# Splitting the first load of a streaming kernel between two issuing engines

## The chip, the cores and the metric

The kernel runs on one core of a Trainium2 chip. The time is the device time of one execution in microseconds, the median of three runs. The profile is one further execution, recorded by the hardware profiler; its span is a little shorter than the device time (167.1 us against 168.98 us for the same execution).

The engines are named as the profile names them: PE is TensorE, with PEld its weight loads, DVE is VectorE, ACT is ScalarE, POOL is GpSimd, and SP is SyncE, which issues the loads. A "q" after an engine's name means its instruction queue.

## The reference

For an input of 32 x 512 rows of 1024 positive numbers, the result is the sum of the reciprocals of each row:

```python
def setup_inputs():
    batch, seq, dim = 32, 512, 1024
    return {"x": np.abs(np.random.randn(batch, seq, dim)).astype(np.float32) + 1e-6}

def reference(x):
    return np.sum(1.0 / x, axis=-1).astype(np.float32)
```

The input is 67.1 MB, the output 64 KB.

## The kernel before

The 16384 rows are spread over 128 partitions, 128 rows each. A row is halved, and two numbers share one reciprocal: 1/a + 1/b = (a + b) x 1/(ab). GpSimd (or VectorE) makes the products, ScalarE makes the reciprocal as exp(-ln), TensorE or the reducing instruction makes the sums, and VectorE multiplies and reduces. A ring of 40 rows per partition holds the input; a hand-made list, PLAN, sets the order of everything. `D4` in it is a load of the next four rows, `D8` of the next eight, and so on.

```python
P = 128; D = 1024; H = D // 2; F = 128; R = 40
PLAN = """
    D4 D8 D15 D13 P0+2 C3@3 S2@0 V3 P2 L0@0 L1@1 C11@3 S3@1 E0@6 E1@7 P4+2 V11 L2@3 L3@2
    R0 S6@2 E2 E3 R1 P6+2 ...                          # cut
""".split()

x_v = x.flatten_outer_dims().rearrange("(p f) d -> p f d", p=P)

act_sets = list(get_activation_tables(nc.m.arch).keys())
nc.scalar.add_instruction(mybir.InstLoadActFuncSet(...))   # cut: ln and exp in one table
...
ring = pool.tile([P, R, D], f32)
...
with tc.manual_schedule():
    for op, r, n, b in ops:
        if op == "D":
            n, r = r, loaded
            while n:
                q, at, w = place(r)
                a = q % R
                m = min(n, R - a, LAST - r) if r < LAST else 1
                inst = nc.sync.dma_start(
                    out=ring[:, a : a + m, at : at + 2 * w],
                    in_=x_v[:, q : q + m, at : at + 2 * w],
                )
                note("SP", inst, writes=rows(r, m))
                r, n = r + m, n - m
            loaded = r
        elif op == "P":      # products on GpSimd, reads the ring
        elif op == "C":      # TensorE copies half a row to PSUM
        elif op in "WV":     # products on VectorE
        elif op == "S":      # TensorE adds the two halves of a row into PSUM
        elif op == "L":      # ScalarE: ln
        elif op == "E":      # ScalarE: exp
        elif op == "R":      # VectorE: multiply and reduce; frees the row of the ring
        # cut
    nc.sync.dma_start(out=out_v, in_=sums)
```

`note` records what an instruction reads and writes, and leaves out a wait that other waits already imply:

```python
def note(engine, inst, reads=(), writes=()):
    ...                                               # cut: finds earlier users of the same rows
    for other in needed:
        o_inst, o_engine, o_tick, _, _, o_known = other
        if o_engine == engine:
            continue
        if o_tick <= known.get(o_engine, 0):
            tc.declare_no_dep(inst, o_inst, reason="implied by other waits")
            continue
        for e, t in o_known.items():
            known[e] = max(known.get(e, 0), t)
        known[o_engine] = max(known.get(o_engine, 0), o_tick)
```

In the built program the loads use eight completion semaphores in turn, so a load also waits until the earlier load with the same semaphore has landed.

Of the kernel before, what the change touches and what calls it, by code (L numbers as in the profile page):

```python
# [11 lines left out]
def kernel(  # L12
# [5 lines left out]
    nc = tc.nc  # L18
    f32 = mybir.dt.float32
    P = 128  # L20
# [58 lines left out]
    x_v = x.flatten_outer_dims().rearrange("(p f) d -> p f d", p=P)  # L79
    out_v = out.flatten().rearrange("(p f) -> p f", p=P)  # L80

    act_sets = list(get_activation_tables(nc.m.arch).keys())
    nc.scalar.add_instruction(  # L83
        mybir.InstLoadActFuncSet(
            name=nc.get_next_instruction_name(),
            act_func_set_id=act_sets.index("natural_log_exp_and_others"),
            ins=[],
            outs=[],
        )
    )  # L90

    pool = ctx.enter_context(tc.tile_pool(name="pool", bufs=1))
    pspool = ctx.enter_context(
        tc.tile_pool(name="pspool", bufs=1, space=bass.MemoryType.PSUM)
# [1 line left out]
    ring = pool.tile([P, R, D], f32)  # L96
# [15 lines left out]
    def place(r):  # L112
        if r < LAST:
            return r, 0, H
        part, q = divmod(r - LAST, F - LAST)
        return LAST + q, part * H, H // 2

    def xs(r, h):
        q, at, w = place(r)
        return ring[:, q % R, at + h * w : at + (h + 1) * w]  # L120

    loaded = 0
# [10 lines left out]
    def note(engine, inst, reads=(), writes=()):  # L133
        inst = inst.ins
        known = dict(begun.get(engine, {}))
        before = {}
        for spaces, writing in ((reads, False), (writes, True)):
            for space in spaces:
                for other in history.get(space, ()):
                    if writing or other[3]:  # L140
                        before[other[0].name] = other
        needed = sorted(before.values(), key=lambda o: -o[4])
# [4 lines that stand above are left out]
            if o_tick <= known.get(o_engine, 0):  # L147
                tc.declare_no_dep(inst, o_inst, reason="implied by other waits")
                continue
            for e, t in o_known.items():  # L150
                known[e] = max(known.get(e, 0), t)
            known[o_engine] = max(known.get(o_engine, 0), o_tick)
        count[engine] = count.get(engine, 0) + 1
        begun[engine] = known
        entry = (engine, count[engine])
        if engine == "SP":
            entry = (f"load {count[engine]}", 1)
        for spaces, writing in ((reads, False), (writes, True)):
            for space in spaces:
                history.setdefault(space, []).append(  # L160
                    (inst, *entry, writing, sum(count.values()), known)
                )

    def rows(r, n, h=None):
        spaces = []
        for q, at, w in (place(i) for i in range(r, r + n)):
            end = at + 2 * w
            if h is not None:
                at, end = at + h * w, at + (h + 1) * w
            spaces += [("row", q % R, i) for i in range(at, end, H // 2)]  # L170
        return spaces

    def slots(r, n):
        return [("slot", pslot[q]) for q in range(r, r + n)]

    with tc.manual_schedule():
        for op, r, n, b in ops:
            p = pslot.get(r)
# [3 lines that stand above are left out]
                    q, at, w = place(r)  # L182
                    a = q % R
                    m = min(n, R - a, LAST - r) if r < LAST else 1
                    inst = nc.sync.dma_start(  # L185
                        out=ring[:, a : a + m, at : at + 2 * w],
                        in_=x_v[:, q : q + m, at : at + 2 * w],
                    )
                    note("SP", inst, writes=rows(r, m))
                    r, n = r + m, n - m  # L190
                loaded = r
            elif op == "P":
                while n:
                    q, at, w = place(r)
                    a, p = q % R, pslot[r]
                    m = min(n, R - a)
                    inst = nc.gpsimd.tensor_tensor(  # L197
                        out=prod[:, p : p + m, :w],
                        in0=ring[:, a : a + m, at : at + w],
                        in1=ring[:, a : a + m, at + w : at + 2 * w],  # L200
                        op=mult,
                    )
                    note("POOL", inst, rows(r, m), slots(r, m))
                    r, n = r + m, n - m
            elif op == "C":
                copied[r] = b
                inst = nc.tensor.matmul(  # L207
                    ps[:, b, : place(r)[2]],
                    lhsT=ident,
                    rhs=xs(r, 1),  # L210
                    start=True,
                    stop=True,
                )
                note("PE", inst, rows(r, 1, 1), [("bank", b)])
            elif op in "WV":
                w = place(r)[2]
                in1 = xs(r, 1) if op == "W" else ps[:, copied[r], :w]
                inst = nc.vector.tensor_tensor(  # L218
                    out=prod[:, p, :w], in0=xs(r, 0), in1=in1, op=mult
                )  # L220
                if op == "W":
                    read = rows(r, 1)
                else:
                    read = rows(r, 1, 0) + [("bank", copied[r])]
                note("DVE", inst, read, slots(r, 1))
            elif op == "S":
                bank[r] = b
                halves.add(r)
                for h in range(2):
                    inst = nc.tensor.matmul(  # L230
                        ps[:, b, : place(r)[2]],
                        lhsT=ident,
                        rhs=xs(r, h),
                        start=h == 0,
                        stop=h == 1,
                    )
                    note("PE", inst, rows(r, 1, h), [("bank", b)])
            elif op == "L":
                pg = prod[:, p : p + n, : place(r)[2]]
                inst = nc.scalar.activation(out=pg, in_=pg, func=Ln, scale=S)  # L240
                note("ACT", inst, writes=slots(r, n))
            elif op == "E":
                pg = prod[:, p : p + n, : place(r)[2]]
                rc = pg
                if b is not None:
                    rc = ps[:, b : b + n, : place(r)[2]]
                    for j in range(n):
                        bank[r + j] = b + j
                inst = nc.scalar.activation(out=rc, in_=pg, func=Exp, scale=-1.0)  # L249
                if b is None:  # L250
                    note("ACT", inst, writes=slots(r, n))
                else:
                    banks = [("bank", b + j) for j in range(n)]
                    note("ACT", inst, slots(r, n), banks)
            elif op == "R":
                q, at, w = place(r)
                other = ps[:, bank[r], :w]
                if r in halves:
                    row = prod[:, p, :w]
                else:  # L260
                    row = ring[:, q % R, at : at + 2 * w]
                    row = row.rearrange("p (h e) -> p h e", h=2)
                    other = other.unsqueeze(1).to_broadcast([P, 2, w])
                total = sums[:, q : q + 1]
                inst = nc.vector.tensor_tensor_reduce(  # L265
                    out=row,
                    in0=row,
                    in1=other,
                    scale=S,
                    scalar=total if q in summed else 0.0,  # L270
                    op0=mult,
                    op1=add,
                    accum_out=total,
                )
                summed.add(q)
                note(
                    "DVE",
                    inst,
                    [("bank", bank[r])],
                    slots(r, 1) if r in halves else rows(r, 1),  # L280
                )
        nc.sync.dma_start(out=out_v, in_=sums)
# [30 lines left out]
```

## Time and profile before

| | before |
|---|---|
| median of 3 runs | 169.06 us (168.96 to 169.12) |
| span of the profiled execution | 167.1 us |
| PE, DVE, ACT, POOL busy | 81%, 77%, 80%, 77% |
| read from HBM | 67.11 MB, 402 GB/s over the span |
| first issue of a load | 0.74 us |
| table load on ACT | 0.73 us, takes 1.28 us |
| first product on POOL, first matmul on PE | 8.12 us, 8.18 us |
| last load issued, output issued | 153.6 us, 164.6 us |

The profile page has a row for the DMA engines in 40 equal slices of the span, the digit being the busy share in tenths. The chain of waits follows what ended last back to the start. In the timeline each line is a start, a duration, the engine, the source line and the operation; the bracket tells how long the engine was idle before it and what ended that. The windows view has, for each stretch, its length, the busy time of PE, PEld, DVE, ACT and POOL with their numbers of instructions, the granted TensorE clock, the mean share of the DMA engines, and GB/s; a packet is counted in the window in which it starts, so short windows can show a share over 1. The packet records, below the views, give start, duration and size of each packet on a DMA engine.

### The profile page before, as it was taken

To read this page: it belongs to the slowest core of one execution; us is meant where nothing else is said; L and a number is where in the kernel's file an instruction comes from. 1 tells how busy PE (TensorE), PEld (TensorE's weight loads), DVE (VectorE), ACT (ScalarE), POOL (GpSimd) and SP (SyncE) were. 2 spreads that over 40 slices of the span, in tenths; PEclk is the share of its full clock that TensorE was granted. 3 is DMA by queue.
4 is the path that set the end of the run, shared out by engine and by line. 5 is a ranking of instruction groups with operands and counts; after the bars stand their busy time and mean duration, and the time that the engine had idled before them with its cause. 6 is when DMAs were issued, how large, how long until landed. Compare 5 with 4: busy or idle time off the path is not lost.

```text
span 167.1 us, 1335 instructions
## 1 busy us (share of the span) xinstructions
PE 135.1 (81%) x292; PEld 55.7 (33%) x292; DVE 128.2 (77%) x283; ACT 133.0 (80%) x161; POOL 128.0 (77%) x80
## 2 busy tenths in 40 slices
PE   0092799039999999977998999999699669989692
PEld 0030343023444334323333434434244133424261
DVE  0010298604789989886798898799999999999994
ACT  3045159207999999977999997999899999999992
POOL 1070792039999999939999997966899997979970
PEclk9999599965999999999999999999999999999999
DMA  5998999999999998999998989999999999999910
GB/s 192 435 502 377 471 471 471 471 408 408 408 408 407 439 466 377 441 424 439 412 471 384 479 377 447 416 449 412 422 428 429 405 432 408 428 408 409 396 64 16
DMA packets 4760, 67.26 MB, mean 403 GB/s; under 512 B 528, under 2 KB 656, under 8 KB 2192
## 3 DMA queue, kind: packets, MB, share of 16 engines
q1 hardware_dynamic: 4752, 67.18, 94.8%
q8 instruction: 2, 0.03, 0.1%
q14 instruction: 6, 0.05, 0.1%
HBM read 67.11 MB, written 0.07 MB: 402 GB/s over the span
## 4 chain that ended last, share of the span: by engine, by line
DMA 60%; DVE 16%; PE 15%; issue 3%; ACT 2%; SPq 1%; DVEq 0%; ACTq 0%
DMA ring<-in_x_dram 60%; PE ps L230 11%; DVE ring L265 10%; DVE prod L265 4%; PE ps L207 4%; DVE prod L218 2%; ACT prod L240 1%; DVE sums L265 1%; ACT prod L249 1%; ACT ps L249 1%; SPq L185 1%; DVEq L308 0%; ACTq L240 0%
## 5 line engine op out<-in xcount | busy, mean ns | idle before, releaser
L197 POOL TENSOR_TENSOR prod<-ring 128x1024 f32<-128x1024 f32 (+2 forms) x74 | 127.3, 1752 | 33.6 <-DMA ring<-in_x_dram 31.6
L230 PE MATMUL ps<-ring,ident 128*128 128x512 f32 (+1 forms) x260 | 118.6, 605 | 4.3 <-DVE sums L265 3.1
L240 ACT ACTIVATE prod<-prod 128x1024 f32<-128x1024 f32 (+2 forms) x80 | 69.0, 876 | 27.0 <-POOL prod L197 26.2
L265 DVE CUSTOM_DVE_ANT_1 ring<-ring,ps 128x1024 f32<-128x1024 f32 (+1 forms) x65 | 76.3, 1209 | 8.4 <-ACT ps L249 8.4
L230 PEld LDWEIGHTS ps<-ring,ident 128*128 128x128 f32 x260 | 49.8, 197 | 72.7 <-issue 51.7
L265 DVE CUSTOM_DVE_ANT_0 prod<-prod,ps 128x512 f32<-128x512 f32 (+1 forms) x63 | 40.7, 678 | 1.4 <-ACT prod L249 1.3
L207 PE MATMUL ps<-ring,ident 128*128 128x512 f32 x32 | 19.9, 712 | 24.5 <-DMA ring<-in_x_dram 24.5
L249 ACT ACTIVATE ps<-prod 128x1024 f32<-128x1024 f32 (+2 forms) x40 | 33.9, 854 | 2.5 <-DVE sums L265 1.8
L249 ACT ACTIVATE prod<-prod 128x1024 f32<-128x1024 f32 (+2 forms) x40 | 34.6, 874 | 0.8
L218 DVE TENSOR_TENSOR prod<-ring,ps 128x512 f32<-128x512 f32 x16 | 10.9, 685 | 26.6 <-PE ps L207 26.4
L207 PEld LDWEIGHTS ps<-ring,ident 128*128 128x128 f32 x32 | 5.9, 212 | 35.1 <-issue 16.3
L265 DVE DVE_READ_ACCUMULATOR2_ANT sums<- 128x1 f32 x130 | 10.7, 82 | 0.0
L218 DVE TENSOR_TENSOR prod<-ring 128x512 f32<-128x512 f32 (+1 forms) x7 | 4.5, 661 | 0.0
L83 ACT ACT_TABLE_LOAD x1 | 1.3, 1283 | 0.7 <-PEq L297 0.7
L265 DVE CUSTOM_DVE_ANT_0 prod<-prod,ps,sums 128x256 f32<-128x256 f32 x2 | 0.9, 478 | 0.0
masks.py:197 POOL MEMSET ident<- 128x128 f32 x1 | 0.2, 204 | 0.3 <-POOLq L297 0.3
masks.py:199 POOL TENSOR_SCALAR_AFFINE_SELECT ident<-ident 128x128 f32<-128x128 f32 x1 | 0.3, 292 | 0.1
L297 POOL MEMSET const-float32-0.0<- 128x1 f32 x1 | 0.1, 99 | 0.2 <-issue 0.2
L297 POOL MEMSET const-bfloat16-1.0<- 128x1 bf16 x1 | 0.1, 102 | 0.0
L297 POOL MEMSET const-uint8-127<- 128x1 uint8 x1 | 0.1, 102 | 0.0
L297 POOL MEMSET const-float32-1.0<- 128x1 f32 x1 | 0.1, 99 | 0.0
## 6 DMA issues: line engine op xcount, KB each, us to landing
ring<-in_x_dram SPq DMA_DIRECT2D x3, 4096.0 KB, 31.5
ring<-in_x_dram SPq DMA_DIRECT2D x4, 2048.0 KB, 34.4
ring<-in_x_dram SPq DMA_DIRECT2D x1, 7680.0 KB, 34.2
ring<-in_x_dram SPq DMA_DIRECT2D x2, 3584.0 KB, 32.3
ring<-in_x_dram SPq DMA_DIRECT2D x1, 6656.0 KB, 49.5
ring<-in_x_dram SPq DMA_DIRECT2D x2, 3072.0 KB, 32.6
ring<-in_x_dram SPq DMA_DIRECT2D x1, 5120.0 KB, 27.2
ring<-in_x_dram SPq DMA_DIRECT2D x4, 1024.0 KB, 30.3
```

What stands on the lines that cost most here:

```text
L83: nc.scalar.add_instruction(mybir.InstLoadActFuncSet(name=nc.get_next_instruction_name(), act_func_set_id=act_sets.index("natural_log_exp_ ...
L185: inst = nc.sync.dma_start(out=ring[:, a : a + m, at : at + 2 * w], in_=x_v[:, q : q + m, at : at + 2 * w],)
L197: inst = nc.gpsimd.tensor_tensor(out=prod[:, p : p + m, :w], in0=ring[:, a : a + m, at : at + w], in1=ring[:, a : a + m, at + w : at + 2 * w],
L207: inst = nc.tensor.matmul(ps[:, b, : place(r)[2]], lhsT=ident, rhs=xs(r, 1), start=True, stop=True,)
L218: inst = nc.vector.tensor_tensor(out=prod[:, p, :w], in0=xs(r, 0), in1=in1, op=mult)
L230: inst = nc.tensor.matmul(ps[:, b, : place(r)[2]], lhsT=ident, rhs=xs(r, h), start=h == 0, stop=h == 1,)
L240: inst = nc.scalar.activation(out=pg, in_=pg, func=Ln, scale=S)
L249: inst = nc.scalar.activation(out=rc, in_=pg, func=Exp, scale=-1.0)
L265: inst = nc.vector.tensor_tensor_reduce(out=row, in0=row, in1=other, scale=S, scalar=total if q in summed else 0.0, op0=mult, op1=add, acc ...
L297: nc = _bacc.Bacc("TRN2", target_bir_lowering=False, num_devices=1)
```

## The change

The first load, of four rows, is made as two transfers of 64 partitions: SyncE issues the one for partitions 0 to 63, ScalarE the one for 64 to 127. ScalarE's table load is moved behind its transfer, so that the transfer goes out first. The purpose is that two engines prepare the first transfer at once and the data begin to flow sooner. All other loads stay as they are. Both halves are recorded as loads of the same rows, and `note` gets a line so that neither is left out as implied by the other; the readers of these rows wait for both.

```diff
-    act_sets = list(get_activation_tables(nc.m.arch).keys())
-    nc.scalar.add_instruction(
-        mybir.InstLoadActFuncSet(
-            ...
-        )
-    )
@@ note
+            if engine == "SP" and o_engine.startswith("load"):
+                continue
             for e, t in o_known.items():
@@ op == "D"
-                    inst = nc.sync.dma_start(
-                        out=ring[:, a : a + m, at : at + 2 * w],
-                        in_=x_v[:, q : q + m, at : at + 2 * w],
-                    )
-                    note("SP", inst, writes=rows(r, m))
+                    step = P if loaded else P // 2
+                    for p0 in range(0, P, step):
+                        queue = nc.scalar if p0 else nc.sync
+                        inst = queue.dma_start(
+                            out=ring[p0 : p0 + step, a : a + m, at : at + 2 * w],
+                            in_=x_v[p0 : p0 + step, q : q + m, at : at + 2 * w],
+                        )
+                        note("SP", inst, writes=rows(r, m))
+                    if not loaded:
+                        act_sets = list(get_activation_tables(nc.m.arch).keys())
+                        nc.scalar.add_instruction(
+                            mybir.InstLoadActFuncSet(
+                                ...
+                            )
+                        )
```

More of the change, by code (lines that the diff above doesn't have):

```diff
@@ L80 @@
     out_v = out.flatten().rearrange("(p f) -> p f", p=P)
-    act_sets = list(get_activation_tables(nc.m.arch).keys())
-    nc.scalar.add_instruction(
-        mybir.InstLoadActFuncSet(
[L85 to L88, printed above, removed]
-        )
-    )
     pool = ctx.enter_context(tc.tile_pool(name="pool", bufs=1))
@@ L184 @@
                     m = min(n, R - a, LAST - r) if r < LAST else 1
-                    inst = nc.sync.dma_start(
-                        out=ring[:, a : a + m, at : at + 2 * w],
-                        in_=x_v[:, q : q + m, at : at + 2 * w],
-                    )
-                    note("SP", inst, writes=rows(r, m))
+                    step = P if loaded else P // 2
[10 more added lines that the diff above has]
+                            mybir.InstLoadActFuncSet(
+                                name=nc.get_next_instruction_name(),
+                                act_func_set_id=act_sets.index("natural_log_exp_and_others"),
+                                ins=[],
+                                outs=[],
+                            )
+                        )
                     r, n = r + m, n - m
```

## The prediction

> **What bounds the kernel now.** I read the page's row of slices first, then the queue table, the chain of waits, and the start of the timeline.
>
> ```profile
> DMA  5998999999999998999998989999999999999910
> GB/s 192 435 502 377 471 471 471 471 408 408 408 408 407 439 466 377 441 424 439 412 471 384 479 377 447 416 449 412 422 428 429 405 432 408 428 408 409 396 64 16
> ...
> q1 hardware_dynamic: 4752, 67.18, 94.8%
> ...
> DMA 60%; DVE 16%; PE 15%; issue 3%; ACT 2%; SPq 1%; DVEq 0%; ACTq 0%
> ```
>
> The DMA engines are full from the second slice (4.2 us) to the 38th (159 us); no slice between is under 8 tenths. The sixteen engines' one hardware queue holds 94.8% of their time. The other engines stand at 77 to 81% of the span. So the kernel is one continuous stream of 67 MB with some 6 us of computing after it. The windows view gives the rate of that stream, and its end:
>
> ```profile
> 10.00:50.00 40.00, 28.93 (x54) 11.58 (x53) 20.72 (x44) 23.52 (x27) 23.96 (x13) 0.87 1.01 436
> 50.00:100.00 50.00, 46.90 (x105) 18.71 (x103) 44.97 (x99) 46.67 (x47) 47.43 (x24) 1.00 0.99 426
> 100.00:150.00 50.00, 45.01 (x102) 18.50 (x102) 47.95 (x104) 47.81 (x62) 42.50 (x30) 1.00 1.00 423
> 150.00:157.00 7.00, 6.10 (x14) 2.35 (x14) 7.00 (x18) 6.82 (x12) 6.93 (x6) 1.00 1.02 407
> 157.00:160.00 3.00, 2.41 (x6) 1.22 (x7) 3.00 (x7) 2.94 (x6) 2.94 (x3) 1.00 0.79 294
> ```
>
> The last two columns are DMA share and GB/s: share about 1.00 throughout. A packet of 16 KB takes 0.611 us in the packet records, so sixteen engines can do 16 x 16384 B / 0.611 us = 429 GB/s, and the windows show that they do. Every load lands when the stream has reached it. The chain of waits agrees; it holds three long pieces of DMA, which are mostly time in the queue:
>
> ```profile
> 1.65 34.24 DMA ring<-in_x_dram
> ...
> 60.27 31.53 DMA ring<-in_x_dram
> ...
> 99.64 35.17 DMA ring<-in_x_dram
> ```
>
> The end therefore moves one for one with whatever shifts the stream as a whole. The start is the one part of the stream that is not full:
>
> ```profile
> 1.50:2.00 0.50, 0.00 (x0) 0.00 (x0) 0.00 (x0) 0.50 (x1) 0.00 (x0) 1.00 1.28 262
> 2.00:2.50 0.50, 0.00 (x0) 0.00 (x0) 0.00 (x0) 0.01 (x1) 0.00 (x0) 1.00 0.45 131
> 2.50:3.00 0.50, 0.00 (x0) 0.00 (x0) 0.00 (x0) 0.00 (x0) 0.00 (x0) 1.00 0.54 197
> 3.00:3.50 0.50, 0.00 (x0) 0.00 (x0) 0.00 (x0) 0.00 (x0) 0.00 (x0) 1.00 1.12 459
> ```
>
> Packets are counted in the window where they start. The sixteen engines' first packets start one after another, from 1.76 to 2.66 us (0.91 us from first to last), and end between 2.93 and 3.44 us, on average at 3.18. Taking 0.611 us off, the stream starts in effect at 2.57 us on average, 1.8 us after SyncE's first issue at 0.74. That is all the change can work on.
>
> [...]
>
> **The change part by part.**
>
> 1. Descriptors of the first load. Before, SyncE issues one load of 128 runs of 16 KB in 0.38 us; now SyncE and ScalarE each issue 64. If the stagger of 0.91 us[...] grows with their number, half of it takes 0.45 us. The mean start of the first packets (2.13 us now) then falls by some 0.15 us[...]. I take 0.3 us earlier, an estimate from these two bounds.[...]
>
> 2. SyncE's next issues. The load of eight rows is issued at 1.18 us[...]. Its first packet starts at 7.19 us, right behind the first load, so nothing comes of it.
>
> 3. Table load. It starts at 0.73 us and ends at 2.01; behind an issue of some 0.4 us it ends at about 2.4. ScalarE's first computation is at 10.49 us. Cost 0.
>
> 4. First readers. GpSimd's first multiply and TensorE's first matmul now wait on two completions. In the built program these are the only waits added on computing engines[...]. If ScalarE's half lags by one packet while SyncE's 32 KB packets have begun (1.213 us each), the first rows come 1.2 us late. The work on them runs from 8.1 to 14.7 us, and then every engine waits for the second load:
>
> ```profile
> 8.12 3.57 POOL L197 TENSOR_TENSOR prod<-ring 128x1024 f32<-128x1024 f32 x2 [6.81 <-DMA ring<-in_x_dram]
> ...
> 13.62 1.13 ACT L249 ACTIVATE prod<-prod 128x512 f32<-128x512 f32 x2
> 17.81 4.67 POOL L197 TENSOR_TENSOR prod<-ring 128x1024 f32<-128x1024 f32 x2 [6.13 <-DMA ring<-in_x_dram]
> ```
>
> ScalarE has 3 us of air there; a late first load is hidden, an early one gives nothing by itself. Only the shift of the stream counts.
>
> 5. Completion semaphores. There are eight, used in turn, and one more load at the front means that SyncE waits for its own load seven before instead of eight. This is the wait of the second line here:
>
> ```profile
> SPq L185 <- DVE sums L265: 98.3, 16, 23.6
> SPq L185 <- DMA ring<-in_x_dram: 42.0, 15, 6.8
> ```
>
> From 114.2 us on it binds: the load issued at 114.167 us follows the landing, eight loads before, at 114.085. Seven deep, it would issue at 121.3, but loads already queued then last until 143.5 us, 22 us of work. The last load would issue at about 154.8 instead of 153.6 us; the fastest engine finishes the load ahead of it at 158.6. The queue doesn't run dry: later issues, same landings. Cost 0.
>
> 6. The added line in the recording of dependencies only keeps both halves as separate things to wait for. The order of instructions is otherwise unchanged.
>
> Sum of the favoured way: 169.06 - 0.3 = 168.8 us.
>
> **Rivals.** (a) [...] Against it: two queues offer both halves at once[...]. (b) Nothing:[...] the engines start as before: 169.0 to 169.1. (c) The queue runs dry with seven loads outstanding: some tenths of a us late. Against it speak the queued times of step 5.
>
> **Range and chances.** I give the favoured way 55%, (b) 15%, and (a) in some degree 30%, a quarter of that at over 3.4 us, which is the 2% line. A gain of 2% would need 3.4 us at the start, and the stream has only 2.57 us ahead of it. The predicted time is 168.8 us, 8 in 10 between 168.2 and 171.2; faster 0.01, same 0.91, slower 0.08.
>
> **What would show it.** Step 1: first packets starting within about 0.5 us, a mean of their ends under 3.18 us, and the second load landing before 17.74 us by the same amount as the end moves. Step 3: no wait of ScalarE on the table load. Step 5: the waits of SyncE on loads grow from 42.0 us, while the DMA share stays about 1.00 up to 157 us. Rival (a): packets of 16 KB that take clearly over 0.611 us in the first 8 us, and a second load landing well after 17.74 us. Rival (b): the same second landing within 0.1 us. I am wrong altogether if the second load lands earlier and the end does not: then a chain of computing, not the stream, sets the end.

## The result and the profile after

The changed kernel takes 174.25 us (median of 4 runs, 173.35 to 174.59) against 169.09 us before (4 runs, 168.96 to 169.13). The ratio is 1.0298, with a 95% interval of 1.0259 to 1.0338: slower by 5.2 us. The profiled execution is the quickest of the four, 173.35 us with a span of 171.4 us, so its trace shows 4.3 us of the loss.

The page after, in the rows that were shown of before:

```profile
DMA  5999979999998999999999998999999999999920
GB/s 134 233 291 443 496 330 459 459 459 398 398 547 356 423 471 459 386 421 435 424 413 466 398 466 378 434 424 449 405 421 428 418 428 410 426 404 409 397 82 15
...
q1 hardware_dynamic: 4688, 66.13, 92.2%
q10 hardware_dynamic: 80, 1.05, 2.7%
...
DMA 31%; DVE 27%; issue 13%; POOL 12%; ACT 8%; PE 7%; SPq 0%; DVEq 0%; POOLq 0%; ACTq 0%
```

The busy share of the DMA engines looks as good as before: the digits don't tell that anything is wrong. The row of GB/s does: its first three slices have 134, 233 and 291, where before had 192, 435 and 502. The engines are as busy as before and move half. ScalarE's queue, q10, carries 1.05 MB, which is one half of the first load; these 1.6% of the bytes take 2.7 of the 94.9 percentage points of the engines' time. The chain's DMA share falls from 60% to 31% although the stream is later. The chain follows one path, and in this profile it stands in computing from 106 us on, where before it left the loads only at 135 us; and 9.87 us that GpSimd waits before the third load lands at 40.20 us are counted under "issue". So this row doesn't tell what was lost. The next view does.

The windows view, before and after, with DMA share and GB/s in the last two columns. Before:

```profile
2.50:5.00 2.50, 0.00 (x0) 0.00 (x0) 0.00 (x0) 0.00 (x0) 0.00 (x0) 1.00 0.90 374
5.00:7.50 2.50, 0.00 (x0) 0.00 (x0) 0.00 (x0) 0.00 (x0) 0.00 (x0) 1.00 1.21 518
7.50:10.00 2.50, 1.82 (x2) 0.84 (x3) 0.00 (x0) 0.00 (x0) 1.88 (x1) 1.00 1.03 446
```

After:

```profile
2.50:5.00 2.50, 0.00 (x0) 0.00 (x0) 0.00 (x0) 0.11 (x1) 0.00 (x0) 1.00 0.93 216
5.00:7.50 2.50, 0.00 (x0) 0.00 (x0) 0.00 (x0) 0.00 (x0) 0.00 (x0) 1.00 0.92 216
7.50:10.00 2.50, 0.00 (x0) 0.00 (x0) 0.00 (x0) 0.00 (x0) 0.00 (x0) 1.00 1.08 249
10.00:12.50 2.50, 0.00 (x0) 0.00 (x0) 0.00 (x0) 0.00 (x0) 0.00 (x0) 1.00 0.93 269
12.50:15.00 2.50, 1.33 (x2) 0.83 (x3) 0.00 (x0) 0.00 (x0) 1.35 (x1) 1.00 0.98 419
```

With all sixteen engines busy, 216 to 249 GB/s pass, 269 in the window in which the first load ends, and 419 after it. The packet records give the same in packets. Sorted by start, sixteen at a time, with the median duration of each sixteen:

```
packets 16 KB each   before: queue, us     after: queue, us
 1st sixteen         SyncE   1.08          SyncE   1.07
 2nd                 SyncE   0.61          SyncE   1.17
 3rd                 SyncE   0.61          ScalarE 1.14
 4th                 SyncE   0.61          SyncE   1.11
 5th                 SyncE   0.61          ScalarE 1.11
 6th                 SyncE   0.61          SyncE   1.11
 7th                 SyncE   0.61          ScalarE 1.11
 8th                 SyncE   0.61          ScalarE 1.24
```

The sixteen engines work on SyncE's half together, then on ScalarE's half, and so on: sixteen of one queue in each row. From the third row on the starts of a row are spread over 0.7 to 0.8 us, so while a row begins, the last engines are still on the row before it, mostly on the other half; the turns overlap. On average the eighth packet ends at 11.27 us instead of 7.46. The timeline after:

```profile
0.73 0.56 ACTq L182 DMA_DIRECT2D ring<-in_x_dram  x1
0.74 2.20 SPq L182 DMA_DIRECT2D ring<-in_x_dram  x4
...
1.33 1.28 ACT L189 ACT_TABLE_LOAD   x1 [1.33 <-PEq L304]
13.65 3.57 POOL L204 TENSOR_TENSOR prod<-ring 128x1024 f32<-128x1024 f32 x2 [12.34 <-DMA ring<-in_x_dram]
...
22.13 2.35 POOL L204 TENSOR_TENSOR prod<-ring 128x1024 f32<-128x1024 f32 x1 [4.91 <-DMA ring<-in_x_dram]
```

The first product starts at 13.65 us instead of 8.12. GpSimd still waits 4.91 us for the second load, so that delay by itself is hidden. But the second load lands at 22.06 us instead of 17.74, 4.3 us later, the third at 40.20 instead of 35.89, also 4.3, and the end is 4.3 us later. The stream lost time once, in its first 13 us (the ninth sixteen end 4.21 us late on average), and never got it back.

### The profile page after: what moved, and what is told of

It is laid out like the page before. It is cut to its first block, busy times and chain, and to the rows that moved or that the text cites. A ratio compares the mean times of both kernels' runs of the same rounds, so it can differ in the third digit from the quotient of the medians.

```text
span 171.4 us, 1338 instructions
## 1 busy us (share of the span) xinstructions
PE 135.2 (79%) x292; PEld 56.1 (33%) x292; DVE 128.3 (75%) x283; ACT 132.8 (77%) x161; POOL 128.1 (75%) x80
## 3 DMA queue, kind: packets, MB, share of 16 engines
q10 hardware_dynamic: 80, 1.05, 2.7%
## 4 chain that ended last, share of the span: by engine, by line
DMA 31%; DVE 27%; issue 13%; POOL 12%; ACT 8%; PE 7%; SPq 0%; DVEq 0%; POOLq 0%; ACTq 0%
DMA ring<-in_x_dram 31%; DVE ring L272 17%; POOL prod L204 12%; DVE prod L272 6%; PE ps L237 5%; ACT prod L247 3%; DVE prod L225 3%; ACT ps L256 3%; PE ps L214 2%; ACT prod L256 1%; DVE sums L272 1%; SPq L182 0%; DVEq L315 0%; POOLq L204 0%; ACTq L247 0%
```

## The experiments

My theory was that the partitions written decide: packets into 0 to 63 or 64 to 127 are slow, like the 1.11 to 1.24 us above, while the engines stand on one half in step, and packets into 32 to 95 take 0.61 us. It was a conjecture, and no trace here shows a reason for it. Where an expectation sets cases side by side, the first is this theory's, but for the two attempts at the end. Rivals were a cost of changing between two queues, two issuers that hinder each other, slowness of any transfer of 64 partitions, and the read side. The landing of the second load (the third where the second was halved too) measures the stream's loss, apart from the rest of the kernel:

| run | packets of the first load | second load lands, us (before 17.74) | span, us (before 167.1) | median, us | ratio, 95% interval |
|---|---|---|---|---|---|
| one queue, halves | 16 KB, 1.05 to 1.28 us | 22.71 | 172.0 | 173.96 | 1.0291, 1.0268 to 1.0313 |
| two queues, rows | 8 KB, 0.31 us | 18.00 | 167.5 | 169.14 | 1.0003, 0.9993 to 1.0014 |
| middle half | 16 KB, half 0.61, half 1.14 to 1.25 | 20.86 | 170.1 | 172.03 | 1.0171, 1.0152 to 1.0190 |
| twelve rows | 16 KB 1.0 to 1.3, 32 KB 2.2 to 2.6 | third 50.71 (35.89) | 181.7 | 183.70 | 1.0861, 1.0833 to 1.0890 |
| small packets | 4 KB, 0.16, then 0.22 to 0.30 | 21.14 | 171.1 | 172.58 | 1.0211, 1.0194 to 1.0228 |
| the change again | 16 KB, 1.0 to 1.28 | 23.07 | 172.5 | 174.35 | 1.0313, 1.0298 to 1.0329 |
| table load first | 16 KB, 1.0 to 1.28 | 23.08 | 172.5 | 174.12 | 1.0306, 1.0291 to 1.0322 |
| into the middle | 16 KB, half 0.61, half 1.15 to 1.24 | 21.52 | 170.8 | 171.98 | 1.0182, 1.0153 to 1.0212 |
| from the middle | 16 KB, 1.16 to 1.29 | 22.93 | 172.6 | 174.23 | 1.0304, 1.0281 to 1.0327 |
| four single rows | 4 KB, 0.16 | 17.93 | 167.6 | 169.35 | 1.0018, 1.0011 to 1.0025 |
| one row and three | 4 and 12 KB, 0.16 and 0.46 | 17.71 | 167.1 | 169.01 | 0.9996, 0.9988 to 1.0005 |

The packets are medians of sixteen, past the first sixteen. In every row the landing's delay and the span's agree within 0.7 us: the end follows the stream. The twelve rows were run twice, the two runs with exchanged sources three times, the others four times or more.

**One queue.** Both halves are issued by SyncE, the second behind the first:

```diff
-                        queue = nc.scalar if p0 else nc.sync
+                        queue = nc.sync
```

> Both halves from SyncE, one behind the other, no second queue. [...] the first load's 16 KB packets still take 1.1 to 1.2 us, the second load lands at 21.7 to 22.3 us, 173.5 to 174.6 us. Queue theory (changing between two queues costs about 0.5 us a packet): packets of 0.61 us, second load at 17.7 us, 169.0 to 169.3 us.

The windows view of this run:

```profile
5.00:7.50 2.50, 0.00 (x0) 0.00 (x0) 0.00 (x0) 0.00 (x0) 0.00 (x0) 1.00 0.96 210
7.50:10.00 2.50, 0.00 (x0) 0.00 (x0) 0.00 (x0) 0.00 (x0) 0.00 (x0) 1.00 1.01 210
```

Without a second queue the engines are full at 210 GB/s, and the time is 173.96 us. The packets take up to 1.28 us, a little more than I expected, and the second load lands at 22.71 us, 0.4 us past my range. The cost of changing queues has fallen as the cause, and so have two issuers at once. The first issue, to 64 partitions, takes 0.56 us here too, alone, against 0.38 us for the first load before; the first packet starts at 2.08 us.

**Two queues, whole rows.** Each queue takes two rows of all 128 partitions:

```diff
-                    step = P if loaded else P // 2
-                    for p0 in range(0, P, step):
-                        queue = nc.scalar if p0 else nc.sync
+                    half = m if loaded else m // 2
+                    for r0 in range(0, m, half):
+                        queue = nc.scalar if r0 else nc.sync
                         inst = queue.dma_start(
-                            out=ring[p0 : p0 + step, a : a + m, at : at + 2 * w],
-                            in_=x_v[p0 : p0 + step, q : q + m, at : at + 2 * w],
+                            out=ring[:, a + r0 : a + r0 + half, at : at + 2 * w],
+                            in_=x_v[:, q + r0 : q + r0 + half, at : at + 2 * w],
                         )
-                        note("SP", inst, writes=rows(r, m))
+                        note("SP", inst, writes=rows(r + r0, half))
```

> Two queues as in the change, but each transfer has two rows of all 128 partitions. [...] 8 KB packets of about 0.31 us, second load at 17.4 to 18.1 us, 168.8 to 169.5 us. Queue theory: half a us lost at each change of queue, second load at 20 us or later, 171 us or more. [...] the first packets start at 2.07 us as after the change, second load at about 18.1 us, 169.4 us.

```profile
0.73 0.40 ACTq L182 DMA_DIRECT2D ring<-in_x_dram  x1
0.74 2.08 SPq L182 DMA_DIRECT2D ring<-in_x_dram  x4
...
1.16 1.28 ACT L189 ACT_TABLE_LOAD   x1 [1.16 <-PEq L304]
8.35 3.58 POOL L204 TENSOR_TENSOR prod<-ring 128x1024 f32<-128x1024 f32 x2 [7.05 <-DMA ring<-in_x_dram]
```

This timeline has what the change has besides the halves: two queues, the table load behind the transfer, the rule in `note`. One thing more differs: each transfer is recorded for its own two rows, so a reader of one row waits for one of the two transfers and not for both. Its ratio of 1.0003 shows that these parts together cost nothing that can be measured. Two issuers at once need 0.40 and 0.38 us, and the first packet starts at 1.75 us as before. So the last of the three cases expected, that two issuers at once start the stream late, has fallen: the late start, 2.07 us in the change and 2.08 with one queue, comes with the halves. But the split brings nothing either. Taking full speed off the mean end of the first packets, as the prediction did, the stream starts in effect at 2.62 us, against 2.57 before.

**The middle half.** One queue, partitions 32 to 95 first:

```diff
-                    step = P if loaded else P // 2
-                    for p0 in range(0, P, step):
-                        queue = nc.scalar if p0 else nc.sync
+                    parts = [(0, P)] if loaded else [(32, 96), (0, 32), (96, 128)]
+                    for p0, p1 in parts:
+                        ...    # nc.sync, partitions p0 to p1 of both sides
```

> One queue, three transfers: partitions 32 to 95, then 0 to 31, then 96 to 127. [...] their 64 packets take 0.61 us each, and the 64 of the outer quarters 1.1 us; half of the loss, second load at 19.7 to 20.4 us, 171.0 to 172.0 us. If any transfer of 64 partitions is slow by itself: 1.1 us for the middle ones too, second load at 22 us, 174 us. Queue theory: 169.0 to 169.3 us.

```profile
3.00:5.00 2.00, 0.00 (x0) 0.00 (x0) 0.00 (x0) 0.00 (x0) 0.00 (x0) 1.00 0.89 377
5.00:7.00 2.00, 0.00 (x0) 0.00 (x0) 0.00 (x0) 0.00 (x0) 0.00 (x0) 1.00 1.11 287
7.00:9.00 2.00, 0.00 (x0) 0.00 (x0) 0.00 (x0) 0.00 (x0) 0.00 (x0) 1.00 1.08 238
```

A transfer of 64 partitions ran at full speed when they were 32 to 95, 0.61 us a packet past the first sixteen, and at about half speed when they were 0 to 63, up to 1.28 us on one queue. Once the outer quarters come, from 5.7 us on, the rate falls to 238 GB/s. What counted is which partitions, not how many. Nor did packets become slow because their load was slow to issue: the middle half took 0.62 us to issue, more than the slow lower half with 0.56. The time is 0.03 us over the range expected and the landing 0.5 us, 0.4 of which is a later first packet (2.15 us instead of 1.75).

**Into the middle, from the middle.** The middle half differs from the lower half on both sides, in the input's addresses as well. Two runs take the sides apart. They exchange the source of the first load between partitions (so the sums of the first four rows of a partition come out at other places, with the same work). Against the run with the middle half:

```diff
-                    parts = [(0, P)] if loaded else [(32, 96), (0, 32), (96, 128)]
+                    parts = [(0, P, 0)] if loaded else [(32, 96, 0), (0, 32, 64), (96, 128, 96)]
+                    # from the middle: [(0, 64, 32), (64, 96, 0), (96, 128, 96)]
-                            in_=x_v[p0:p1, q : q + m, at : at + 2 * w],
+                            in_=x_v[s0 : s0 + p1 - p0, q : q + m, at : at + 2 * w],
```

> As the run with the middle half, but the source is exchanged: partitions 32 to 95 of the ring are written from the input rows of partitions 0 to 63, 0 to 31 from those of 64 to 95 (the first four rows' sums come out at other places). If the write side is what is narrow: the first 64 packets take 0.61 us, the rest 1.1 to 1.3, second load at 20.5 to 21.1 us, 171.7 to 172.3 us, as with the middle half. If the read side is (addresses of the input's first half): 1.1 to 1.3 us for the first 64 packets.

> The other way round: partitions 0 to 63 of the ring are written from the input rows of partitions 32 to 95, then 64 to 95 from those of 0 to 31, then 96 to 127 from their own (again the first four sums come out at other places). Write side: 1.1 to 1.3 us for the first 64 packets and the rest, second load at 22.4 to 23.1 us, 173.7 to 174.5 us. Read side: 0.61 us for the first 64 packets, about 172 us.

Windows of the run that writes to the middle, from the lower half of the input:

```profile
3.00:5.00 2.00, 0.00 (x0) 0.00 (x0) 0.00 (x0) 0.00 (x0) 0.00 (x0) 1.00 0.83 352
```

and of the run that writes to 0 to 63, from the middle of the input:

```profile
3.00:5.00 2.00, 0.00 (x0) 0.00 (x0) 0.00 (x0) 0.00 (x0) 0.00 (x0) 1.00 1.21 262
5.00:7.00 2.00, 0.00 (x0) 0.00 (x0) 0.00 (x0) 0.00 (x0) 0.00 (x0) 1.00 0.79 164
```

Past the first sixteen, the first transfer's packets take 0.61 us into the middle and 1.17 to 1.28 from the middle. The speed went with the partitions that are written; the addresses that are read didn't matter. The first of the two lands its second load 0.4 us past my range; both times are in it. That settles the write side.

**Twelve rows.** The second load is halved too:

```diff
-                    step = P if loaded else P // 2
+                    step = P if loaded >= 12 else P // 2
```

> The second load, of eight rows, is halved between the two queues too, so three times the bytes. [...] the 12 rows move at about 236 GB/s, 26.6 us in place of 14.7, so the loss is 12 to 14 us: 181 to 184 us, 32 KB packets of about 2.2 us, the third load landing at 47 to 50 us. If the loss is a fixed cost of starting two queues: 174 to 175 us.

The 236 GB/s expected is an estimate from the change's packets, 16 x 16384 B / 1.11 us. Three times the bytes cost 14.6 us against 5.2. The third load lands at 50.71 us, 0.7 us past my range, and the packets of 32 KB take up to 2.6 us, more than the 2.2 us expected; the time is in its range. A fixed cost of starting two queues has fallen; the loss goes with the bytes moved in halves.

**Small packets.** Each half in four transfers of one row, in turn on the two queues:

```diff
+                    parts = [(0, P, 0, m)]
+                    if not loaded:
+                        parts = [(p0, p0 + 64, j, 1) for j in range(m) for p0 in (0, 64)]
+                    for p0, p1, j, k in parts:      # row j alone, from p0 to p1
+                        ...    # and recorded as a load of row j alone
```

> The two queues and the two halves of the change, but each half in four transfers of one row, so packets of 4 KB, 0.153 us at full speed. The engines start up to 0.7 us apart, now several packets. If the loss needs the engines to be on the same half in step, many are on opposite halves here: packets between 0.16 and 0.30 us, less loss than the change, 170 to 172.5 us. If two halves serialize whatever the engines do, or if the loss is one per change of queue (now 4 times as many changes): 174 us or more.

With 172.58 us the loss is 3.6 us, just over the range I gave. Here sixteen packets in succession are mostly no longer of one queue, but anything from 15 and 1 to 8 and 8, and they take 0.22 to 0.30 us, between one and two times 0.153. I had expected that of engines which are partly on opposite halves. But the sixteen that were 8 and 8 still took 0.22 us, and two that were 9 and 7 took 0.24 and 0.28, so a mixture of queues by itself didn't restore full speed, and no run here tells what would. It isolates nothing either: the packets' size and the number of issues changed with it. What it does show is that halves on two queues needn't lose the 5.2 us of the change: 3.6 were lost here.

**The change again, and with the table load first.**

> The changed kernel once more, for a second profile of the first load. [...] 173.3 to 174.6 us, and the span follows the duration of the 16 KB packets: with packets of 1.1 us a span of 171.4 us as before, with 1.2 to 1.25 us one of 172.2 to 172.6 us.

> One part undone: ScalarE's table load stands ahead of its half of the load again, which is then issued 0.6 to 1.3 us later. [...] the loss stays: 173.5 to 174.6 us. If ScalarE's issue beside SyncE's were the cause (two issuers at once), most of it goes: under 171 us.

In the second profile of the change the engines took all four of SyncE's packets of the half before they turned to ScalarE's queue, whose packets then alternated with those of SyncE's second load. The packets took up to 1.28 us, the second load landed at 23.07 us, and the span is 172.5 us. So the order in which engines served the two queues differed between these two executions, and the second landing by a microsecond; that fits the spread of 173.35 to 174.59. That the order makes this difference is not shown by two profiles.

Moving the table load back has a surprise:

```profile
0.73 1.28 ACT L181 ACT_TABLE_LOAD   x1 [0.73 <-PEq L304]
...
0.73 2.27 SPq L192 DMA_DIRECT2D ring<-in_x_dram  x4
0.76 0.57 ACTq L192 DMA_DIRECT2D ring<-in_x_dram  x1
```

ScalarE's queue issues the transfer at 0.76 us, while the table load runs. I had expected it 0.6 to 1.3 us late. Putting the transfer first, as the change does, issues it 0.02 us sooner; the loss stays. As the issue came hardly later, this run says little about two issuers at once; the single queue had settled that.

**What the change was for, without halves.** Two attempts on the kernel before, in the plan alone, with 128 partitions and SyncE only:

```diff
-        D4 D8 D15 D13 ...
+        D1 D1 D1 D1 D8 D15 D13 ...      # four single rows
+        D1 D3 D8 D15 D13 ...            # one row and three
```

> An attempt at what the change was for, without halves: the kernel before, its first load of four rows made as four transfers of one row, all 128 partitions, all from SyncE (packets of 4 KB). The first 4 KB packets of the small-packet run took 0.35 us on average. If smaller first packets let the stream start sooner: its effective start falls from 2.57 to 2.1 to 2.4 us, second load at 17.3 to 17.6 us, 168.6 to 168.9 us. If the start is set by the 1.0 us from issue to the first packet and the stagger of the engines: 168.9 to 169.3 us.

> The same with two transfers, of one row and of three. If the size of the first packet is what counts: as with four transfers of one row, 168.6 to 168.9 us. Otherwise 168.9 to 169.3 us.

Four single rows take 169.35 us, 0.05 us past the second of the two ranges, and are 0.2% slower: 4 KB packets take 0.159 us each, where a quarter of 0.611 would be 0.153, and the second load lands at 17.93 us. One row and three lands it at 17.71 us, and the time is the same (interval 0.9988 to 1.0005). No version here beats the kernel before.

## Why the prediction was wrong

The step that failed is the argument against rival (a), packets that take clearly over 0.611 us: "two queues offer both halves at once". With it I kept full speed for the first load, 8 x 0.611 = 4.9 us for an engine's eight packets. From the second on they took 1.11 to 1.24 us each (medians of sixteen), and the eighth ended at 11.27 us instead of 7.46. The halves were on offer together, but the engines took the same half in the same turn, sixteen packets of one queue in each row of the table. Whether that is why the two queues didn't make up for the slow halves stays open, since the mixed packets of the small-packet run were slow too; that the halves themselves are slow is shown by the run with one queue, at 1.05 to 1.28 us a packet.

The bound was read rightly. The stream sets the end, and its shift passes on whole: 4.32 us at the second landing, 4.3 at the end. Steps 3 and 6 cost nothing, as the run with whole rows shows. Step 4 had the late first rows hidden behind the wait for the second load, and so they were, though they came 5.5 us late and not 1.2.

Step 1 had the wrong sign. I took half of the partitions for half of the issuing work and counted "0.3 us earlier". The issue took 0.56 us instead of 0.38, the first packet started at 2.07 us instead of 1.76, and the first sixteen ended at 3.36 us on average instead of 3.18: 0.2 us later. Two issuers at once weren't the reason: alone on one queue a half took 0.56 us to issue too, and two whole transfers from two queues took 0.40 and 0.38. The second load was issued at 1.36 us instead of 1.18, without effect.

Step 5 had no effect, but its reasoning was wrong too. I had each of SyncE's loads wait for the one seven before. One more load at the front shifts the semaphore of every later load alike, so a later load still waits for the load eight before, and only the eighth load from SyncE gets a wait that it didn't have. SyncE's waits after:

```profile
SPq L182 <- DVE sums L272: 102.3, 15, 27.9
SPq L182 <- DMA ring<-in_x_dram: 41.9, 15, 6.8
```

These are 41.9 us against 42.0; I had said that they would grow.

So rival (a) decided. What it foretold came about: packets of 1.11 to 1.24 us instead of 0.611, and a second landing at 22.06 us instead of 17.74. I gave it 30%, and only a quarter of that to a loss of over 3.4 us, where 5.2 was measured; these weights were my estimate, as no load of the trace before goes to 64 partitions. The profile before held a hint: all engines start within 0.91 us and then run packets of equal length, 0.611 us, which shows nothing that would set them apart. That is a reading after the fact; no run here changed the step of the engines and nothing else. The range, up to 171.2 us, was too low for the same reason.

In rates, the packets give 16 x 16384 B / 1.28 us = 205 GB/s on one queue, and with 1.106 us 237 GB/s where the engines alternate between the halves, against 429 before. The runs show which partitions written were slow, 0 to 63 and not 32 to 95; none shows why.

## What to carry to other kernels

If a transfer has to be split, split it by rows, not into the halves 0 to 63 and 64 to 127: the partitions written decided the speed here, 1.05 to 1.28 us for 16 KB in halves against 0.31 us for 8 KB by rows, and a second queue didn't make up for it. Read the DMA share together with GB/s and the duration of packets of a known size; from 7.5 to 10 us a share of 1.08 stood beside 249 GB/s here, where before 1.03 stood beside 446. In this kernel, which streams without a gap, the 4.32 us lost at the second landing were 4.3 lost at the end, so weigh a small hoped-for gain there against the worst that a new shape of transfer can do.

## What was unexpected of the hardware

- Issuing the first load took longer to 64 partitions than to 128: 0.56 us in the change and with one queue, 0.62 us for the middle half, against 0.38 us before, on either engine, alone or beside another. Its first packet starts at 2.07 to 2.15 us instead of 1.75. The number of partitions isn't all of it: the second load, to all 128, took 0.56 us to issue behind a half in the changed kernel, and 0.42 before. Why is open.
- 64 partitions were not slow as such: 32 to 95 took 0.61 us for a 16 KB packet, 0 to 63 took 1.05 to 1.28, whichever addresses were read.
- ScalarE's queue issued a load 0.03 us after the start of a table load of 1.28 us that stood ahead of it.
- In the small-packet run the second and third packets of 4 KB still ran at about full speed, 0.16 us, before they slowed to 0.22 to 0.30. Why is open.
- Two executions of the same program served the two queues in a different order; their second landings are 1.0 us apart.
